# A four-part decoder trunk on one core: 224 bytes in front of the left side of SBUF

## The chip, the core and the metric

The kernel runs on one core of a Trainium2 chip. The metric is the device time of one execution in microseconds (us), the median of several. Engines are named as in the profile: PE (TensorE) does the matmuls, PEld is its weight load, DVE (VectorE) and ACT (ScalarE) work element by element, POOL is GpSimd, and SP issues most DMAs from its queue, in order.

## The reference

One sequence of 1024 tokens, width 1024, float32, goes through two layers. Every layer is a pre-normalised mixer and a pre-normalised SwiGLU FFN (2816 wide), both added to x. The mixer of layer 0 is a forgetting attention of 8 heads beside a causal pooling of 4 channel groups; that of layer 1 is RWKV-7 time mixing: three large projections, three small ones, a recurrence over 16 heads of 64, a norm per head and an output projection.

```python
for layer in range(DEPTH):                       # DEPTH = 2
    h = _rmsnorm(x, mix_norm[layer])
    y = _fox_pool_mixer(h, ...) if layer % 2 == 0 else _rwkv7_time_mix(h, ...)[0]
    x = x + y
    x = x + _swiglu(_rmsnorm(x, ffn_norm[layer]), ffn_w_gate[layer], ffn_w_up[layer], ffn_w_down[layer])
```

## The kernel before, in words

Activations lie transposed, channels on partitions, in tiles of 128 x 512: eight channel blocks for each of two halves of the tokens. A wide product is done in three (`mm3`, L162 to L164): weights and activations are each split into a rounded part and a rest (hi and lo), and hi*hi, hi*lo and lo*hi are added up in PSUM. Each of the three streams a moving tile of 512 columns through a stationary block of 128 x 128 weights. Tiles are named by what they hold: `whi`, `wlo` are weights, `hh` and `hl`, `uh` and `ul`, `h1h` and `h1l`, `mxh` and `mxl`, `gh` and `gl` are the two parts of an activation. `load_part` (L149 to L151) brings weights in: a DMA from the SP queue into `wraw`, a cast on ACT for hi, a subtraction on DVE for lo.

SBUF is used as two stacks that grow towards each other. The left one begins with constants (`setup`: cc, cv, eps, hlast, om, nb, bones) and holds pools opened and closed in order; the right one begins at the far end with `wf`, the pool of weights. Pools of the left side are x0, h (hh, hl of the attention), wl and u (uh, ul: the first FFN and the first dense projection), core and core2 (the recurrence), tail0 and tail1 (hh, hl, gh, gl of the last FFN), and w4, a weight pool for the last stage. Pools of the right side are wf (whi, wlo, wraw for all stages but the last), x1, fox (the attention), t1, m1 (h1h, h1l) and mb (mxh, mxl of the second dense projection). In the listing the side is the second argument of `pool`. A tile's size is rounded up to a multiple of 32 bytes.

The stages in order of time, in the profiled execution: attention and pooling (to about 490 us); the output projection, the first FFN and the first dense projection (490 to 1090); the first recurrence, into whose gaps the rest of the FFN is woven as `fm` from h1 (1090 to 1590); the second dense projection (1590 to 1790); the second recurrence, woven with the last FFN of the first half as `fm` from h and g (1790 to 2290); the last FFN (2290 on). `weave` writes out the order by hand: matmuls of the recurrence stand at fixed places among those of the fill, and PE takes them in that order. A number yielded by `job` says how many matmuls of fill go in between.

`open_core` (L931) sets up a recurrence, twice: it loads the masks (msk), the group constants (gc: 32 columns for sums over a head, 128 for the spread matrix, 1 for a sign), casts the spread matrix to a tile of its own on ACT, and sets the state S. `job` then loads s, k, a, r and v (L958) and uses temporaries of tag t2. Both core pools fill their room to within a few hundred bytes.

Of the kernel before, what the change touches and what calls it, by code (L numbers as in the profile page):

```python
# [9 lines left out]
F32 = mybir.dt.float32  # L10
F32R = mybir.dt.float32r
AF = mybir.ActivationFunctionType
ALU = mybir.AluOpType
# [3 lines left out]
P = 128  # L17
# [38 lines left out]
def make_consts():  # L56
    c = np.zeros((P, NCC), np.float32)
    f = np.zeros((P, NFC), np.float32)
    i = np.arange(P)
    same = (i[:, None] // 64) == (i[None, :] // 64)  # L60
    c[:, CC["ident"]:CC["ident"] + P] = np.eye(P)
    c[:, CC["bones"]:CC["bones"] + P] = same / 64.0
    c[:, CC["ones"]:CC["ones"] + P] = 1.0 / D
    c[:, CC["cent"]:CC["cent"] + P] = np.eye(P) - same / 64.0
    f[:, FC["maskT"]:FC["maskT"] + P] = np.where(i[:, None] > i[None, :], NEG, 0.0)
    f[:, FC["maskQ"]:FC["maskQ"] + P] = np.where(i[None, :] > i[:, None], NEG, 0.0)
    for g, w in enumerate((2, 4, 8, 16)):
        f[:, FC["icnt"] + 16 * g:FC["icnt"] + 16 * g + 16] = 1.0 / np.minimum(np.arange(16) + 1, w)
    return c, f
# [11 lines left out]
def rd(ap):  # L81
    return ap.bitcast(F32)


def setup(ctx, tc, k):
    nc = tc.nc
    k.tc, k.nc = tc, nc
    k.const = ctx.enter_context(tc.tile_pool(name="const", bufs=1))
    k.uid = 0
    k.prio, k.cur = {}, 0  # L90
    k.cc = k.const.tile([P, NCC], F32, tag="cc", name="cc")
    k.cv = k.const.tile([P, NCV], F32, tag="cv", name="cv")
    k.eps = k.const.tile([P, 3], F32, tag="eps", name="eps")
    nc.gpsimd.memset(k.eps[:, 0:1], RMS_EPS)
    nc.gpsimd.memset(k.eps[:, 1:2], GN_EPS)
    nc.gpsimd.memset(k.eps[:, 2:3], 1e-35)
    k.hlast = k.const.tile([P, KT], F32, tag="hlast", name="hlast")
    k.om = k.const.tile([P, 48], F32, tag="om", name="om")
    k.nb = k.const.tile([P, 16], F32, tag="nb", name="nb")
    k.bones = k.const.tile([P, P], F32R, tag="bones", name="bones")  # L100
    k.lag2, k.lag3 = 100000, 100000
# [11 lines left out]
def nm(k, s):  # L113
    k.uid += 1
    return f"{s}_{k.uid}"
# [15 lines left out]
def pst(k, tag, bufs):  # L131
    return k.ps.tile([P, HN], F32, tag=tag, name=nm(k, tag), bufs=bufs)
# [608 lines left out]
class Rwkv:  # L741
# [188 lines left out]
    def open_core(self, cp):  # L930
        k, nc = self.k, self.k.nc  # L931
        self.cp = cp
        self.msk = cp.tile([P, 2, 64], F32, tag="msk", name="msk")
        nc.sync.dma_start(self.msk, self.ins["rconst"])
        self.gc = cp.tile([P, 161], F32, tag="gc", name="gc")
        nc.sync.dma_start(self.gc, self.ins["gconst"])
        self.spread = cp.tile([P, P], F32R, tag="spread", name="spread")
        nc.scalar.copy(self.spread, self.gc[:, 32:160])
        self.rst = cp.tile([P, HN], F32, tag="rst", name="rst")
        nc.gpsimd.memset(self.rst, 1.0)  # L940
        nc.gpsimd.memset(self.rst.rearrange("p (c t) -> p c t", t=64)[:, :, 0:1], 0.0)
        self.S = cp.tile([P, 8, 64], F32, tag="S", name=nm(k, "S"))
        s = self.S.rearrange("p a b -> p (a b)")
        if self.last is None:
            nc.gpsimd.memset(s, 0.0)
        else:
            nc.sync.dma_start(s, self.last)
        self.vc = cp.tile([P, 3, 8], F32, tag="vc", name="vc")
        nc.vector.tensor_scalar(self.vc[:, 0], k.cv[:, CV["k_a"]:CV["k_a"] + 8], -1.0, 1.0, ALU.mult, ALU.add)
        nc.vector.tensor_scalar(self.vc[:, 2], k.cv[:, CV["k_k"]:CV["k_k"] + 8], -1.0, None, ALU.mult)  # L950
        nc.vector.tensor_scalar(self.vc[:, 1], k.cv[:, CV["r_k"]:CV["r_k"] + 8], 64.0, None, ALU.mult)
# [32 lines left out]
    def job(self, grp, half):  # L984
# [4 lines left out]
        k, nc, cp = self.k, self.k.nc, self.cp  # L989
# [210 lines left out]
        rs = self.t2("rs")[:, 0:HN]  # L1200
        nc.scalar.activation(rs, z, AF.Ln, bias=k.eps[:, 1:2])
        nc.scalar.activation(rs, rs, AF.Exp, scale=-0.5)
        hi, both = (self.t2(n, F32R)[:, 0:HN] for n in ("hi", "both"))
        nc.scalar.copy(hi, rs)
        nc.vector.scalar_tensor_tensor(both, rd(hi), self.gc[:, 160:161], rs, ALU.mult, ALU.add)
        yield GY[1]
        for i, p in enumerate(pr):
            q = slice(32 * i, 32 * i + 32)
            rs = pst(k, "o", 2)
# [4 lines left out]
            t = self.t2("gn")[:, 0:HN]  # L1214
# [18 lines left out]
def build(ctx, tc, ins, outs, dbg=None, stop=99):  # L1233
    nc = tc.nc
    k = K()
    setup(ctx, tc, k)
    nc.sync.dma_start(k.cv, ins["cvec"])
    nc.vector.tensor_scalar(k.om, k.cv[:, CV["mu0"]:CV["mu0"] + 48], -1.0, 1.0, ALU.mult, ALU.add)
# [220 lines left out]
def layout(inputs):  # L1459

    f = {n: np.ascontiguousarray(v) for n, v in inputs.items()}
    r = {}

    def wb(w):
        kk, m = w.shape
        return np.ascontiguousarray(w.reshape(kk // P, P, m // P, P).transpose(2, 1, 0, 3).reshape(m // P, P, kk))

    def col(v):
        return v.reshape(-1, P).T

    def wl(w):
        n = w.shape[1]
        return np.ascontiguousarray(w.reshape(KT, P, n).transpose(1, 0, 2).reshape(P, KT * n))

    r["xT"] = np.ascontiguousarray(f["x"][0].T)
    r["consts"], r["fconst"] = make_consts()
    cv = np.zeros((P, NCV), np.float32)

    def put(n, v):
        cv[:v.shape[0], CV[n]:CV[n] + v.shape[1]] = v  # L1480

    for n, v in (("mix0", f["mix_norm"][0]), ("ffn0", f["ffn_norm"][0]), ("mix1", f["mix_norm"][1]), ("ffn1", f["ffn_norm"][1]),
                 ("w0", f["rw_w0"][0]), ("a0", f["rw_a0"][0]), ("k_k", f["rw_k_k"][0]), ("k_a", f["rw_k_a"][0]),
                 ("r_k", f["rw_r_k"][0].reshape(-1)), ("ln_w", f["rw_ln_w"][0]), ("ln_b", f["rw_ln_b"][0]),
                 ("pool_scale", f["hy_pool_scale"][0])):
        put(n, col(v))
    for i in range(6):
        put(f"mu{i}", col(f["rw_mu"][0, i]))
    put("q_gain", np.tile(f["hy_q_gain"][0], 2)[:, None])
    put("k_gain", np.tile(f["hy_k_gain"][0], 2)[:, None])  # L1490
    put("f_bias", f["hy_f_bias"][0][:, None])
    r["cvec"] = cv
    w = f["hy_w_in"][0]
    r["w_in"] = wb(np.concatenate([w[:, 0:2048], w[:, 2056:2568]], axis=1))
    r["wf"] = wl(np.pad(w[:, 2048:2056], ((0, 0), (0, 24))))
    r["pool_w"] = f["hy_pool_w"][0]
    r["w_out"] = wb(f["hy_w_out"][0])
    for n in "rkvo":
        r["w_" + n] = wb(f["rw_w_" + n][0])
    i = np.arange(P) % 64  # L1500
    t = np.arange(64)
    j = np.arange(P) % 32
    gc = np.zeros((P, 161), np.float32)
    gc[:, 0:32] = (np.arange(P)[:, None] // 64 == np.arange(32) % 2) / 64.0
    gc[:, 32:160] = (j[:, None] % 2 == np.arange(P) // 64) & (j[:, None] < 4)
    gc[:, 160] = np.where(j // 2 == 1, -1.0, 0.0)
    r["gconst"] = gc
    r["rconst"] = np.stack([i[:, None] < t, i[:, None] <= t], axis=1).astype(np.float32)

    r["w1"], r["a1"] = wl(f["rw_w1"][0]), wl(f["rw_a1"][0])  # L1510
    r["g1a"], r["g1b"] = wl(f["rw_g1"][0][:, 0:P]), wl(f["rw_g1"][0][:, P:])
    r["w2"], r["a2"] = np.tile(f["rw_w2"][0], (2, 1)), np.tile(f["rw_a2"][0], (2, 1))
    r["g2a"], r["g2b"] = np.ascontiguousarray(f["rw_g2"][0][0:P]), np.tile(f["rw_g2"][0][P:], (3, 1))
    for l in range(2):
        r[f"wg{l}"] = wb(f["ffn_w_gate"][l])
        r[f"wu{l}"] = wb(f["ffn_w_up"][l])
        r[f"wd{l}"] = np.ascontiguousarray(f["ffn_w_down"][l].reshape(NFB, P, 8, P).transpose(2, 1, 0, 3))
    return r
# [29 lines left out]
```

## Time and profile before

| | us |
|---|---|
| median of 3 runs (lowest, highest) | 2719.55 (2719.53, 2722.38) |
| profiled execution, its own time | 2725.7 |
| its span | 2723.9 |

Over the span PE is busy 98%, PEld 76%, DVE 63%, ACT 48%, POOL 2%. In the profile a busy PE counts each matmul from its start to its modelled end; neighbours overlap, so the distance from start to start says how fast they follow each other, not the duration. Idle time in a row is the engine's idle time just before the instructions of that row, and behind the arrow stands what ended it.

### The profile page before, as it was taken

The numbers are of one execution on the slowest core, as the hardware profiler recorded it, in microseconds if no ns is written. First come the engines' busy times: TensorE is split into PE (matmuls) and PEld (weight loads), VectorE is DVE, ScalarE is ACT, GpSimd is POOL, SyncE is SP. The second block draws the span as 40 slices with busy tenths as digits, with TensorE's granted clock in tenths as the row PEclk, the third lists the DMA queues.
The fourth block names the chain that finished last, engine by engine and source line by source line (L and its number), as shares of the span: only waits on it lengthen the run. The fifth ranks groups of instructions, "written<-read, shape, count | busy, mean of one in ns | idle before, by whom it ended". The sixth has DMA issues, their size and how long they took to land.

```text
span 2723.9 us, 40262 instructions
## 1 busy us (share of the span) xinstructions
PE 2665.5 (98%) x15368; PEld 2080.5 (76%) x15368; DVE 1725.1 (63%) x2940; ACT 1297.9 (48%) x2297; POOL 50.0 (2%) x139
## 2 busy tenths in 40 slices
PE   9999999999999999999999999999999999999999
PEld 6777778778888777777777677777777777788887
DVE  7777684653336655975995676569769856544443
ACT  7555564442224766534644467655445344333232
POOL 1000000000001000000000000000000000000000
PEclk9999999999999999999999999999999999999999
DMA  4111131233333445423533534454344236333332
GB/s 134 57 51 57 41 96 51 82 93 94 94 96 112 159 164 179 132 88 95 175 93 98 185 105 154 163 184 128 90 136 136 86 98 201 104 97 97 97 97 93
DMA packets 170241, 306.11 MB, mean 112 GB/s; under 512 B 18608, under 2 KB 25904, under 8 KB 170048
## 3 DMA queue, kind: packets, MB, share of 16 engines
q1 hardware_dynamic: 156224, 278.38, 32.8%
q10 hardware_dynamic: 13824, 25.17, 2.5%
q8 instruction: 120, 1.97, 0.3%
q14 instruction: 73, 0.60, 0.1%
HBM read 257.04 MB, written 46.43 MB: 111 GB/s over the span
## 4 chain that ended last, share of the span: by engine, by line
PE 82%; DVE 11%; ACT 3%; DMA 2%; issue 2%; SPq 0%; ACTq 0%; DVEq 0%
PE mm L162 17%; PE mm L163 16%; PE mm L164 16%; PE fm L162 7%; PE fm L164 6%; PE fm L163 6%; DVE wlo L151 2%; PE mm L174 1%; DVE nu L1109 1%; DVE pd L1107 1%; PE s L1057 1%; PE o L1174 1%; PE s L1162 1%; PE s L1168 1%; PE o L1187 1%
## 5 line engine op out<-in xcount | busy, mean ns | idle before, releaser
L150 ACT CAST whi<-wraw 128x512 fp32r<-128x512 f32 x738 | 453.1, 616 | 891.6 <-PE mm L163 493.0
L151 DVE TENSOR_TENSOR wlo<-wraw,whi 128x512 fp32r<-128x512 f32 x738 | 500.9, 683 | 455.9 <-ACT whi L150 445.5
L162 PE MATMUL mm<-hh,whi 128*128 128x512 f32 x864 | 345.1, 401 | 5.8 <-ACT hh L354 5.7
L164 PE MATMUL mm<-hh,wlo 128*128 128x512 f32 x864 | 340.4, 394 | 0.0
L163 PE MATMUL mm<-hl,whi 128*128 128x512 f32 x864 | 339.5, 394 | 0.0
L164 PE MATMUL mm<-uh,wlo 128*128 128x512 f32 x728 | 287.3, 395 | 1.4 <-DVE wlo L151 1.4
L162 PE MATMUL mm<-uh,whi 128*128 128x512 f32 x728 | 287.7, 397 | 0.9 <-DVE x L1315 0.9
L163 PE MATMUL mm<-ul,whi 128*128 128x512 f32 x728 | 287.5, 396 | 0.0
L162 PE MATMUL fm<-h1h,whi 128*128 128x512 f32 x528 | 220.7, 418 | 14.0 <-DVE sg L725 9.9
L163 PE MATMUL fm<-h1l,whi 128*128 128x512 f32 x528 | 210.1, 398 | 0.1
L164 PE MATMUL fm<-h1h,wlo 128*128 128x512 f32 x528 | 209.7, 397 | 0.5 <-DVE wlo L151 0.5
L162 PEld LDWEIGHTS mm<-hh,whi 128*128 128x128 f32 x864 | 162.8, 189 | 42.6 <-ACT hh L354 6.5
L164 PEld LDWEIGHTS mm<-hh,wlo 128*128 128x128 f32 x864 | 162.8, 188 | 35.9 <-DVE wlo L151 0.6
L163 PEld LDWEIGHTS mm<-hl,whi 128*128 128x128 f32 x864 | 163.2, 189 | 33.6 <-DVE hl L259 1.5
L162 PE MATMUL fm<-hh,whi 128*128 128x512 f32 x416 | 174.5, 420 | 3.2 <-ACT hh L258 2.7
L164 PE MATMUL fm<-hh,wlo 128*128 128x512 f32 x416 | 167.9, 404 | 0.0
L163 PE MATMUL fm<-hl,whi 128*128 128x512 f32 x416 | 167.7, 403 | 0.2 <-DVE hl L259 0.2
L162 PEld LDWEIGHTS mm<-uh,whi 128*128 128x128 f32 x728 | 136.4, 188 | 38.7 <-issue 3.5
L163 PEld LDWEIGHTS mm<-ul,whi 128*128 128x128 f32 x728 | 136.6, 188 | 35.8 <-issue 1.1
L164 PEld LDWEIGHTS mm<-uh,wlo 128*128 128x128 f32 x728 | 136.5, 188 | 35.0 <-DVE wlo L151 2.2
L704 DVE TENSOR_TENSOR x<-mm,x 128x512 f32<-128x512 f32 x96 | 66.2, 692 | 122.8 <-PE mm L164 122.5
L162 PEld LDWEIGHTS fm<-h1h,whi 128*128 128x128 f32 x528 | 100.4, 190 | 48.1 <-DVE sg L725 12.3
(338 smaller groups left out, 4642.5 us busy)
## 6 DMA issues: line engine op xcount, KB each, us to landing
wraw<-in_wg_dram SPq DMA_DIRECT2D x176, 256.0 KB, 2.8
wraw<-in_wu_dram SPq DMA_DIRECT2D x176, 256.0 KB, 2.7
wraw<-in_wd_dram SPq DMA_DIRECT2D x176, 256.0 KB, 2.7
wraw<-in_w_in_dram SPq DMA_DIRECT2D x52, 256.0 KB, 2.9
x<-in_xT_dram SPq DMA_DIRECT2D x32, 256.0 KB, 4.6
x<-x SPq DMA_DIRECT2D x32, 256.0 KB, 3.6
wraw<-in_w_k_dram SPq DMA_DIRECT2D x32, 256.0 KB, 2.8
wraw<-in_w_v_dram SPq DMA_DIRECT2D x32, 256.0 KB, 3.0
```

Source lines behind the costliest of these rows:

```text
L150: k.nc.scalar.copy(hi[0:p, 0:n], raw[0:p, 0:n])
L151: k.nc.vector.tensor_tensor(lo[0:p, 0:n], raw[0:p, 0:n], rd(hi[0:p, 0:n]), ALU.subtract)
L162: nc.tensor.matmul(out, wh, xh, start=(first and i == 0), stop=False)
L163: nc.tensor.matmul(out, wh, xl, start=False, stop=False)
L164: nc.tensor.matmul(out, wl, xh, start=False, stop=(last and i == n - 1))
L174: k.nc.tensor.matmul(out[n * q:n * q + n], w[:, n * j:n * j + n], xs[j], start=c == 0, stop=c + g == len(xs), tile_position=(0, n * q))
L704: nc.vector.tensor_tensor(X[half][m], o, X[half][m], ALU.add)
L1057: nc.tensor.matmul(scs[h][:, 128 * c:128 * c + 128], bk[HS[h], 4 * b + c], ZL[h][HS[h], i, 4 * b + c], start=True, stop=True)
L1107: nc.vector.tensor_tensor(pv, nu[:, j + 1:32, j:j + 1].broadcast_to([P, n, j]), nu[:, j:j + 1, 0:j].broadcast_to([P, n, j]), ALU.mult)
L1109: nc.vector.tensor_tensor(nu[:, j + 1:32, 0:j], nu[:, j + 1:32, 0:j], pv, ALU.add)
L1162: nc.tensor.matmul(z[HS[h], i], ZL[h][:, i, c, 0:64], SV[h][:, i, c], start=True, stop=True)
L1168: nc.tensor.matmul(u[HS[h], i], XR[HS[h], i, c, 0:64], zs[HS[h], i], start=True, stop=True)
```

## The change

The eps tile, of which three columns are used, grows from 3 to 64 columns: from 12 bytes, rounded up to 32, to 256. All tiles of the left side behind it (hlast, om, nb, bones and all left pools) move up by 224 bytes; cc, cv and the right side stay. To make room in the core pools, gc keeps 33 columns of its 161 (from 672 bytes after rounding to 160), and the 128 columns of the spread matrix come by a DMA of their own into a temporary of tag t2, from which ACT casts them. The sign column moves from 160 to 32, in the constants and where it is read.

```diff
-    k.eps = k.const.tile([P, 3], F32, tag="eps", name="eps")
+    k.eps = k.const.tile([P, 64], F32, tag="eps", name="eps")
...
-        self.gc = cp.tile([P, 161], F32, tag="gc", name="gc")
-        nc.sync.dma_start(self.gc, self.ins["gconst"])
+        self.gc = cp.tile([P, 33], F32, tag="gc", name="gc")
+        nc.sync.dma_start(self.gc, self.ins["gconst"][:, 0:33])
         self.spread = cp.tile([P, P], F32R, tag="spread", name="spread")
-        nc.scalar.copy(self.spread, self.gc[:, 32:160])
+        t = self.t2("spread")[:, 0:P]
+        nc.sync.dma_start(t, self.ins["gconst"][:, 33:161])
+        nc.scalar.copy(self.spread, t)
...
-        nc.vector.scalar_tensor_tensor(both, rd(hi), self.gc[:, 160:161], rs, ALU.mult, ALU.add)
+        nc.vector.scalar_tensor_tensor(both, rd(hi), self.gc[:, 32:33], rs, ALU.mult, ALU.add)
...
-    gc[:, 32:160] = (j[:, None] % 2 == np.arange(P) // 64) & (j[:, None] < 4)
-    gc[:, 160] = np.where(j // 2 == 1, -1.0, 0.0)
+    gc[:, 33:161] = (j[:, None] % 2 == np.arange(P) // 64) & (j[:, None] < 4)
+    gc[:, 32] = np.where(j // 2 == 1, -1.0, 0.0)
```

## Rows read from the trace of the kernel before

**Rows 1.** The page: busy time of each engine, and the chain that ended last
```profile
PE 2665.5 (98%) x15368; PEld 2080.5 (76%) x15368; DVE 1725.1 (63%) x2940; ACT 1297.9 (48%) x2297; POOL 50.0 (2%) x139
...
PE 82%; DVE 11%; ACT 3%; DMA 2%; issue 2%; SPq 0%; ACTq 0%; DVEq 0%
```
**Rows 2.** Windows by stage: length, busy us (instructions) PE PEld DVE ACT POOL, clock, DMA share, GB/s
```profile
0.00:490.00 490.00, 477.11 (x2217) 376.17 (x2218) 347.85 (x696) 280.86 (x510) 16.64 (x46) 1.00 0.22 68
490.00:1090.00 600.00, 595.76 (x2584) 468.37 (x2583) 311.04 (x479) 277.31 (x467) 13.67 (x26) 1.00 0.38 122
1090.00:1590.00 500.00, 479.33 (x3886) 364.90 (x3885) 381.36 (x654) 235.96 (x438) 8.99 (x30) 0.98 0.39 123
1590.00:1790.00 200.00, 197.02 (x835) 149.77 (x834) 114.93 (x175) 128.64 (x214) 0.15 (x2) 0.99 0.46 149
1790.00:2290.00 500.00, 486.26 (x3969) 368.34 (x3968) 378.28 (x649) 244.13 (x456) 10.59 (x35) 0.99 0.42 130
2290.00:2724.00 434.00, 430.04 (x1886) 352.99 (x1884) 191.64 (x290) 131.04 (x215) 0.00 (x0) 1.00 0.32 100
```
**Rows 3.** Timeline, PE, first FFN: start us, us, instruction; first and last of 19
```profile
699.74 0.40 PE L163 MATMUL mm<-ul,whi 128*128 128x512 f32 x1
...
703.94 0.40 PE L163 MATMUL mm<-ul,whi 128*128 128x512 f32 x1
```
**Rows 4.** Timeline, PE, second dense projection: first and last of 13
```profile
1739.64 0.39 PE L162 MATMUL mm<-mxh,whi 128*128 128x512 f32 x1
...
1742.36 0.39 PE L162 MATMUL mm<-mxh,whi 128*128 128x512 f32 x1
```
**Rows 5.** Timeline, PE, last FFN: first and last of 13
```profile
2449.67 0.39 PE L162 MATMUL mm<-hh,whi 128*128 128x512 f32 x1
...
2452.39 0.39 PE L162 MATMUL mm<-hh,whi 128*128 128x512 f32 x1
```
**Rows 6.** The page's groups: count | busy us, mean ns | idle before, releaser
```profile
L162 PE MATMUL fm<-h1h,whi 128*128 128x512 f32 x528 | 220.7, 418 | 14.0 <-DVE sg L725 9.9
L163 PE MATMUL fm<-h1l,whi 128*128 128x512 f32 x528 | 210.1, 398 | 0.1
L164 PE MATMUL fm<-h1h,wlo 128*128 128x512 f32 x528 | 209.7, 397 | 0.5 <-DVE wlo L151 0.5
...
L162 PE MATMUL fm<-hh,whi 128*128 128x512 f32 x416 | 174.5, 420 | 3.2 <-ACT hh L258 2.7
L164 PE MATMUL fm<-hh,wlo 128*128 128x512 f32 x416 | 167.9, 404 | 0.0
L163 PE MATMUL fm<-hl,whi 128*128 128x512 f32 x416 | 167.7, 403 | 0.2 <-DVE hl L259 0.2
```
**Rows 7.** Groups of 0:490, 490:1090, 1790:2290 (two), 2290:2724 (two): the middle product
```profile
L163 PE MATMUL mm<-hl,whi 128*128 128x512 f32 x441 | 175.0, 398 | 0.0
...
L163 PE MATMUL mm<-ul,whi 128*128 128x512 f32 x728 | 287.5, 396 | 0.0
...
L163 PE MATMUL fm<-hl,whi 128*128 128x512 f32 x324 | 130.6, 403 | 0.0
...
L163 PE MATMUL fm<-gl,whi 128*128 128x512 f32 x132 | 52.5, 398 | 0.0
...
L163 PE MATMUL fm<-gl,whi 128*128 128x512 f32 x44 | 17.3, 397 | 0.0
...
L163 PE MATMUL fm<-hl,whi 128*128 128x512 f32 x24 | 9.5, 395 | 0.0
```
**Rows 8.** Timeline of SP's queue at the first opening and the second
```profile
1063.54 0.42 SPq L936 DMA_DIRECT2D gc<-in_gconst_dram  x1
1064.05 0.38 SPq L958 DMA_DIRECT2D ld<-s  x1
...
1793.72 0.45 SPq L947 DMA_DIRECT2D S<-S  x1
1795.97 0.33 SPq L958 DMA_DIRECT2D ld<-s  x1
```

## The prediction

> **What bounds the kernel now.** I read the busy line and the chain of the page first [rows 1]: TensorE is busy 98% of the span and holds 82% of the chain that ended last, VectorE 11%. So the spacing of its matmuls is the time, unless a stage says otherwise. The table by stage comes next [rows 2]; the reader is to see that TensorE is busy 477 to 480 of 490 to 500 us even in the stages in which the other engines do most (attention, 0:490; the two recurrences, 1090:1590 and 1790:2290), and 596 of 600 and 430 of 434 in the dense stages.
>
> "Busy" is not "at its best" here, and the third view, the timeline, shows it. In the first FFN the wide matmul (128x512) starts every 233.3 ns: 18 steps in 703.94 - 699.74 = 4.20 us [rows 3]. In the second dense projection it starts every 226.7 ns: 12 steps in 2.72 us [rows 4], and in the last FFN again every 226.7 ns [rows 5]. The instruction is the same each time, from the same line, at the same granted clock (1.00 in 490:1090 and 2290:2724 [rows 2]), with no idle time in front of it. What differs is where the two operands lie. In rows 3 the moving tile uh comes from a pool of the left side and the weights whi and wlo from a pool of the right. In rows 4 both come from the right, in rows 5 both from the left (the last stage has weight pool w4, on the left). By the sizes in the code all tiles of one side that hold a wide operand (2048 bytes each; the eight x tiles of a pool, 2080 bytes each, add up to a multiple of 256) stand at one place modulo 256, and the two sides 32 bytes apart: the pad is 256 - 32. So operands at equal places step at 226.7 ns and operands 32 bytes apart at 233.3: 6.6 ns, 2.8%.
>
> The same pair is to be seen where matmuls fill the gaps of a recurrence. There I go by durations, as the starts are mixed with short matmuls: fm from h1 (right side, right weights) takes 418, 398 and 397 ns for its three products, fm from h (left side, right weights) 420, 403 and 404 [rows 6]. That is 2, 5 and 7 ns, on average 4.7 ns. (In the dense stages the duration falls with the spacing, 396 [rows 7] against 389 [rows 4, 5].)
>
> **The change part by part.** The pad moves every left tile after it by 224 bytes. Left moving tiles then stand at the weights' place modulo 256; left weights under left tiles and right under right keep their relation, as both or none move. gc shrinks by 512 bytes, a multiple of 256, so core tiles behind it end at the same new place as the rest. Which matmuls change class, by the rows that count the middle one of three products [rows 7], each times 3:
> - first FFN and first dense projection, 728 x 3 = 2184, at 6.6 ns: 14.4 us. TensorE is continuous there [rows 2], so all of it arrives.
> - end of the FFN, 2290 on, (24 + 44) x 3 = 204, at 6.6 ns: 1.3 us, all of it.
> - attention, 441 x 3 = 1323. No row shows such a matmul at equal places there; the bounds are 0 and 6.6 ns. I take the 4.7 of rows 6, the nearest row in which matmuls are mixed with other work: 6.2 us.
> - second recurrence, (324 + 132) x 3 = 1368, at 4.7 ns: 6.4 us.
> - the rest of fm from h, 416 - 324 - 24 = 68, x 3 = 204, at 4.7 ns: 1.0 us.
>
> Of the last three not all arrives. In the second recurrence VectorE is busy 378 of 500 us [rows 2], and fm from h waits little now (3.2 us over the whole span, 2.7 of them for the split of hh [rows 6]); but the first recurrence, whose fill has the quick placing already, waited 14.0 us on its L162 [rows 6], 9.9 of them for the SwiGLU product of VectorE at L725. I read that as what is late next once the fill is quicker, and let half of the 6.4 arrive: 3.2 us. In attention and the rest I let seven eighths arrive, 6.3 of 7.2, as TensorE idles 13 of 490 us there [rows 2].
>
> Of what matmuls without a wide left operand do, little is known: products with a constant tile ahead of the pad (cc stays where it is) change their distance. By the code there are 4 jobs x 4 head pairs x 16 = 256 short products with cent and as many transposes with ident. They could gain or lose; by 6.6 ns on each this is 3.4 us either way, and as they read an eighth of the columns I take 0.
>
> The other edit costs something. Each open of a core puts one more transfer into SP's queue, between gc and the loads of the recurrence. In the first opening SP issues gc at 1063.54 and ld<-s at 1064.05 [rows 8]: one more issue is about 0.5 us by which ld<-s and all behind it in the queue come later. The target is a t2 tile, which must be free: at the second opening the nearest row of such a wait is ld<-s, 2.3 us behind S<-S with an issue of 0.45 us, thus some 1.8 us of waiting. So 0.5 to 2.3 us each, 0 if the fill (f1's matmuls) covers it. I take 0.5 twice, 1.0 us. ScalarE's copy into spread waits for the new transfer in place of gc's and has the scan's results queued behind it; the scan waits for ld<-s, which is issued later, so the copy holds nothing up.
>
> Sum: 14.4 + 1.3 + 3.2 + 6.3 - 1.0 = 24.2 us off. The profiled execution took 2725.7 us (span 2723.9 and 1.8 around it), so 2701.5, a factor of 0.9911. The runs have their median at 2719.55, 0.2% below that execution; by the same factor they come to 2695.4. I say 2695.
>
> [...]
>
> **The rivals.**
> - Only the continuous stages gain. The mixed stages are bound by the chain of VectorE and ScalarE, and quicker fill is waited away. For it: the 14.0 us of the first recurrence. Against: 82% of the chain is TensorE. 14.4 + 1.3 = 15.7, less 1.0 to 4.6 for the openings, 11 to 15 us off: 2705 to 2708.5.
> - All arrives, at the full 6.6 ns: 2184 + 204 + 1323 + 1368 + 204 = 5283 x 6.6 = 34.9 us off, 2685.
> - The places modulo 256 have nothing to do with it; the two speeds go with the stage or the pool. For it: each class is seen in stages of its own. Against: rows 4 and 5 agree to the tenth of a ns with operands on opposite sides of the memory, other tiles and other DMA shares (0.46 and 0.32 [rows 2]). Then 0 to +5 us: 2720 to 2724.
> [...]
>
> **How the numbers follow.** The forecast 0.61 (2690 to 2701); only the continuous stages 0.20; all at the full rate 0.10; no effect of the place 0.05; the clock 0.04. The range reaches from 2687 (most of the full gain) to 2708 (nearly all of the second case): 0.61 of the first, some 0.17 of the second and some 0.04 of the third, about 0.8. What a measurement of this kernel can tell from no change is 0.2%, 5.4 us. Faster by more: 0.61 + 0.20 + 0.10 = 0.91; within: 0.05; slower: 0.04.
>
> **What would show it.** Right: in the first FFN the starts of L162 to L164 step by 226.7 ns and uh, ul come to 389 to 390 ns; fm from h takes what fm from h1 does; the stage that ended at 1090 ends some 20 us earlier, the last one changes by 1 to 2 us. The first recurrence is as long as before. If uh still steps at 233 ns the main step is wrong; if it steps at 227 and the span does not follow, the handing on is. If ld<-s comes more than 2 us behind gc, the price of the transfer is. [...]

## The result, and the profile after

| | us |
|---|---|
| before, on the same chip: median of 4 runs (the three of before and one more) | 2720.97 |
| after: median of 4 runs (lowest, highest) | 2701.28 (2699.79, 2703.13) |
| ratio, 95% interval | 0.9923 [0.9904, 0.9942] |
| profiled execution of after, its own time | 2699.79 |

The change made the kernel faster by 0.8%, 19.7 us by the medians. The profiled execution went from 2725.7 to 2699.79 us, 25.9 less.

The page of after, its busy line and the chain that ended last, beside [rows 1]:

```profile
PE 2632.5 (98%) x15368; PEld 2072.6 (77%) x15368; DVE 1725.1 (64%) x2940; ACT 1298.7 (48%) x2297; POOL 49.4 (2%) x139
...
PE 77%; DVE 14%; ACT 3%; DMA 3%; issue 3%; SPq 0%; DVEq 0%; ACTq 0%
```

TensorE runs the same 15368 matmuls and is busy 33.0 us less, its weight loads 7.9 less, and the other engines are within 1 us of before. Its share of the chain fell from 82 to 77%, VectorE's rose from 11 to 14%: the kernel is still bound by TensorE, a little less so.

The windows by stage of after (columns as in [rows 2]):

```profile
0.00:490.00 490.00, 476.30 (x2232) 377.91 (x2233) 350.81 (x701) 281.57 (x511) 16.64 (x46) 1.00 0.21 69
490.00:1090.00 600.00, 595.72 (x2705) 478.78 (x2704) 325.76 (x502) 287.63 (x484) 13.33 (x28) 1.00 0.40 125
1090.00:1590.00 500.00, 478.00 (x3844) 365.00 (x3844) 379.81 (x651) 237.94 (x439) 8.04 (x27) 0.99 0.39 123
1590.00:1790.00 200.00, 194.76 (x820) 146.45 (x818) 111.07 (x170) 130.16 (x218) 2.28 (x8) 0.99 0.50 162
1790.00:2290.00 500.00, 483.41 (x3995) 371.69 (x3996) 381.51 (x654) 240.49 (x448) 9.08 (x30) 0.99 0.41 127
2290.00:2698.00 408.00, 404.27 (x1779) 332.78 (x1777) 176.19 (x266) 120.90 (x198) 0.00 (x0) 1.00 0.33 98
```

TensorE is about as full as before in every stage (0.8 to 2.9 us less in those with other work), and in 490:1090 it gets 2705 matmuls done where it did 2584 [rows 2]. The timeline of the first FFN shows why; first and last of 19 wide matmuls, beside [rows 3]:

```profile
700.05 0.39 PE L163 MATMUL mm<-uh,whi 128*128 128x512 f32 x1
...
704.13 0.39 PE L163 MATMUL mm<-uh,whi 128*128 128x512 f32 x1
```

That is 18 steps in 4.08 us: 226.7 ns each, where it was 233.3. The page's groups that answer to [rows 6 and 7]:

```profile
L163 PE MATMUL mm<-uh,whi 128*128 128x512 f32 x728 | 283.5, 391 | 0.9 <-DVE x L1318 0.9
L165 PE MATMUL mm<-uh,wlo 128*128 128x512 f32 x728 | 283.1, 389 | 1.2 <-DVE wlo L152 1.2
...
L163 PE MATMUL fm<-h1h,whi 128*128 128x512 f32 x528 | 218.7, 415 | 14.8 <-DVE sg L726 10.6
L165 PE MATMUL fm<-h1h,wlo 128*128 128x512 f32 x528 | 208.7, 396 | 0.5 <-DVE wlo L152 0.5
L164 PE MATMUL fm<-h1l,whi 128*128 128x512 f32 x528 | 208.5, 395 | 0.1
...
L163 PE MATMUL fm<-hh,whi 128*128 128x512 f32 x416 | 172.4, 414 | 3.5 <-ACT hh L259 2.8
L164 PE MATMUL fm<-hl,whi 128*128 128x512 f32 x416 | 164.5, 396 | 0.2 <-DVE hl L260 0.2
L165 PE MATMUL fm<-hh,wlo 128*128 128x512 f32 x416 | 164.6, 396 | 0.0
```

The fill from h now takes what the fill from h1 takes: 414, 396, 396 ns against 415, 395, 396. Its waits stayed (3.5 us, 3.2 before).

To see where the 26 us went I compared the start of each matmul with that of the same matmul, by its place in PE's order, in the trace of before. The length of a stage is then the distance between the same two matmuls in every kernel. The kernels of the experiments give more values for each stage. "Apart" are those whose left side stands 32 or 128 to 224 bytes off the right one (before, p0, p192, d128_160, d192_16); "equal" are four that keep the pad of 224 bytes (after, t32, lo32, after2). In the first recurrence, the second dense projection and the last FFN most operands are at equal places in both; what changes there is 28, 175 and 52 products of fill from h and g. Kernels that change the last FFN itself are left out of its two rows.

| stage, us | before | after | mean of the kernels apart | mean of those equal | difference |
|---|---|---|---|---|---|
| attention | 483.9 | 480.4 | 484.1 (5) | 480.9 (4) | -3.2 |
| output projection, first FFN, first dense projection | 571.7 | 557.4 | 571.1 (5) | 557.5 (4) | -13.6 |
| first recurrence | 518.7 | 515.1 | 516.5 (5) | 516.2 (4) | -0.3 |
| second dense projection | 211.0 | 210.3 | 211.2 (5) | 210.5 (4) | -0.7 |
| second recurrence | 476.9 | 473.9 | 476.9 (5) | 474.2 (4) | -2.7 |
| start of the last FFN | 79.1 | 78.6 | 79.5 (3) | 78.6 (2) | -0.9 |
| last FFN | 372.5 | 372.3 | 372.5 (3) | 372.3 (2) | -0.2 |

The differences add up to 21.6 us. The profiled pair differs by 4 us more, most of it in the first recurrence (3.6 in place of 0.3), and that goes with the granted clock: TensorE ran part of the stage at 0.50, as the windows 1085:1090 and 1190:1195 of before show. There six steps of the fill from h1, from 1193.30 to 1195.86, take 427 ns each; the median step of that fill at 1.00 is 227. Two longer windows of before (columns as in [rows 2]):

```profile
1060.00:1110.00 50.00, 47.94 (x301) 37.34 (x300) 40.00 (x65) 31.42 (x57) 1.89 (x6) 0.93 0.55 171
...
1160.00:1210.00 50.00, 45.46 (x414) 36.07 (x413) 39.39 (x69) 19.27 (x34) 0.00 (x0) 0.90 0.26 77
```

The same windows of after:

```profile
1060.00:1110.00 50.00, 45.63 (x363) 34.66 (x364) 48.67 (x79) 29.94 (x56) 1.05 (x4) 1.00 0.46 148
...
1160.00:1210.00 50.00, 45.94 (x570) 35.66 (x569) 33.81 (x48) 19.29 (x36) 0.00 (x0) 0.97 0.27 80
```

With 0.50 as the lower level, a mean clock of 0.93 over 50 us is 7 us at it, 0.90 is 10. By the comparison matmul by matmul after gains 1.9 us around the first of these stretches and 2.6 around the second, and loses 0.9 in the rest of the stage. Over the span the time at 0.50 adds up to 44 us in the profile of before and 23 in that of after, and it goes from 21 to 39 us among the kernels below, so single executions scatter widely. But scatter is not all of it: the mean granted clock is 0.9938 over the 29 runs of before beside the experiments and 0.9942 over the 10 of p0, against 0.9952 over the 17 of after, after2, fox and fox2. By twice the missing share of the span that is 32 to 34 us at the lower level against 26. By 427 against 227 ns TensorE loses a little under half of such a time, so, as an estimate, up to 3 or 4 of the 20 us or so gained can have come with the clock; why kernels with the pad were granted more, no run shows. No profile shows the lower level between 14 and 1084 us (before and after have 1.00 in 14:500 and 500:1060, and before then 0.52 in 1084:1091), so the 16.8 us of the first two stages are free of it.

### The profile page after: what moved, and what is told of

It reads as the page before. It is cut to its first block, busy times and chain, and to the rows that moved or that the text cites. A ratio compares the mean times of both kernels' runs of the same rounds, so it can differ in the third digit from the quotient of the medians.

```text
span 2698.0 us, 40269 instructions
## 1 busy us (share of the span) xinstructions
PE 2632.5 (98%) x15368; PEld 2072.6 (77%) x15368; DVE 1725.1 (64%) x2940; ACT 1298.7 (48%) x2297; POOL 49.4 (2%) x139
## 4 chain that ended last, share of the span: by engine, by line
PE 77%; DVE 14%; ACT 3%; DMA 3%; issue 3%; SPq 0%; DVEq 0%; ACTq 0%
PE mm L163 16%; PE mm L164 16%; PE mm L165 16%; PE fm L163 6%; PE fm L164 5%; PE fm L165 5%; DVE wlo L152 2%; PE mm L175 1%; DVE nu L1112 1%; DVE pd L1110 1%; DVE ZL L1068 1%; DMA wraw<-in_wd_dram 1%; DMA wraw<-in_wu_dram 1%; ACT whi L151 1%; PE o L1177 1%
## 5 line engine op out<-in xcount | busy, mean ns | idle before, releaser
L163 PE MATMUL mm<-hh,whi 128*128 128x512 f32 x864 | 343.7, 400 | 6.7 <-ACT hh L355 6.2
L163 PE MATMUL mm<-uh,whi 128*128 128x512 f32 x728 | 283.5, 391 | 0.9 <-DVE x L1318 0.9
L163 PE MATMUL fm<-h1h,whi 128*128 128x512 f32 x528 | 218.7, 415 | 14.8 <-DVE sg L726 10.6
L163 PEld LDWEIGHTS mm<-hh,whi 128*128 128x128 f32 x864 | 162.5, 188 | 43.1 <-ACT hh L355 6.9
L163 PE MATMUL fm<-hh,whi 128*128 128x512 f32 x416 | 172.4, 414 | 3.5 <-ACT hh L259 2.8
L163 PEld LDWEIGHTS mm<-uh,whi 128*128 128x128 f32 x728 | 136.5, 188 | 34.6 <-issue 2.7
L163 PEld LDWEIGHTS fm<-h1h,whi 128*128 128x128 f32 x528 | 99.5, 189 | 48.7 <-DVE sg L726 13.3
```

The lines of the kernel that those rows point to most:

```text
L163: nc.tensor.matmul(out, wh, xh, start=(first and i == 0), stop=False)
```

## The experiments

All but the last two groups ask what makes the step short. Each kernel is the changed one with the edit shown; times of the kernel before are from the same chip.

**Is it the pad, or the other edit?** p0 takes the pad away and keeps the spread transfer and the smaller gc.

```diff
-    k.eps = k.const.tile([P, 64], F32, tag="eps", name="eps")
+    k.eps = k.const.tile([P, 3], F32, tag="eps", name="eps")
```

> The changed kernel with the pad taken out again (eps 3 columns wide) and the other edit left in: gc narrow, the spread matrix by a transfer of its own. Left tiles stand 32 bytes off the weights, as before. If the place is what counts: uh in the first FFN steps at 233.3 ns, the time is that of the kernel before plus 0 to 1 us for the added transfers, ratio 1.000. If the gain came with the other edit (less room taken by gc, another order in SP's queue, fewer stretches at half clock): the time is that of the changed kernel, ratio 0.992, although uh steps at 233.3.

2724.14 us (10 runs) against 2724.44 before, ratio 0.9997 [0.9987, 1.0006]. The timeline of its first FFN, 18 steps in 4.20 us, 233.3 ns again:

```profile
699.27 0.39 PE L163 MATMUL mm<-uh,whi 128*128 128x512 f32 x1
...
703.47 0.39 PE L163 MATMUL mm<-uh,whi 128*128 128x512 f32 x1
```

The whole gain is the pad's, and the other edit costs nothing that can be measured.

**Is it the side, or the place?** t32 leaves the pad and puts 32 bytes in front of the tiles of the last stage, whose moving tiles and weights are both on the left. They are then 32 bytes apart on one side.

```diff
     c_l, lp = pool("tail1")
+    lp.tile([P, 8], F32, tag="pad", name="pad")
```

> The changed kernel, with a tile of 32 bytes in front of pool tail1 (hh, hl, gh, gl of the last FFN), so that in the last stage alone the moving tiles stand 32 bytes off the weights of pool w4, both on the left. If the distance counts: mm from hh and gh steps at 233.3 ns in place of 226.7; (384 + 176) x 3 = 1680 steps x 6.6 ns = 11.1 us more than the changed kernel, all in the last 420 us, ratio to the kernel before 0.9964. If what counts is that operands lie on different sides: no change in the last stage, 226.7 ns, ratio 0.992.

2712.66 us (4 runs), ratio to before 0.9959 [0.9944, 0.9974]; the last FFN took 382.6 in place of 372.3 us. Its timeline, 18 steps in 4.20 us:

```profile
2449.29 0.39 PE L163 MATMUL mm<-hh,whi 128*128 128x512 f32 x1
...
2453.49 0.39 PE L163 MATMUL mm<-hh,whi 128*128 128x512 f32 x1
```

So 32 bytes bring the 233.3 ns to operands of one side, other things equal, and the stage loses 10.3 us. Side and stage fall as explanations.

**Which weights count?** lo32 does the same for the lo weights alone: whi at the moving tiles' place, wlo 32 bytes from it.

```diff
-    hi, lo = ((pool or k.wp).tile([P, w], F32R, tag=tag + i, name=nm(k, tag + i), bufs=bufs or k.wbufs) for i in ("hi", "lo"))
+    wp = pool or k.wp
+    hi = wp.tile([P, w], F32R, tag=tag + "hi", name=nm(k, tag + "hi"), bufs=bufs or k.wbufs)
+    if wp is getattr(k, "padlo", None):
+        wp.tile([P, 56], F32, tag="pad", name="pad")
+        k.padlo = None
+    lo = wp.tile([P, w], F32R, tag=tag + "lo", name=nm(k, tag + "lo"), bufs=bufs or k.wbufs)
...
     c_w, wp4 = pool("w4")
+    k.padlo = wp4
     c_l, lp = pool("tail1")
+    lp.tile([P, 8], F32, tag="pad2", name="pad2")
```

> The changed kernel, with wlo of pool w4 moved down against everything else in the last stage, so that the moving tile stands 32 bytes above wlo (the slow distance) and level with whi. If the moving stream is slowed by the load of the next weights: of three steps only the one from L164 to L165 is 233 ns long (hl streams while wlo is loaded), the others 226.7; 560 steps x 6.6 = 3.7 us over the changed kernel. If it is slowed by the weights that it runs through itself: only the step that starts at L165 is long. If any place off the common one slows all: all three at 233, 11 us.

One run, 2709.22 us; last FFN 379.1 us, 6.8 more than in after. Timeline, 18 steps in 4.16 us, 231.1 ns:

```profile
2448.88 0.39 PE L168 MATMUL mm<-hh,whi 128*128 128x512 f32 x1
...
2453.04 0.39 PE L168 MATMUL mm<-hh,whi 128*128 128x512 f32 x1
```

Over the stage the three steps differ: from hh,whi to hl,whi 226.7 ns, from hl,whi to hh,wlo 235.0, from hh,wlo to the next hh,whi 231.7. The step that is longest is that of hl, which runs through weights at its own place while the 32 bytes distant wlo is being loaded (in the trace of after a load of wlo and the product from gl beside it both start at 2449.28 us, and take 0.19 and 0.39). So the load of the next weights beside the running stream matters. Whether the 231.7 comes from the running stream's own weights or is carried over from the step before isn't told apart; neither figure that I had expected for the stage came out.

**Which distances are quick?** p192 pads 192 bytes (distance 32 the other way). The three others have two distances each: one in the first FFN by the size of eps, one in the last by a pad in tail1 as in t32 (96 and 160 bytes) or, in d192_16, by gh and gl starting 16 bytes into larger tiles.

```diff
# p192, d64_96, d128_160, d192_16: distances 224 (-32), 64, 128, 192 in the first FFN
-    k.eps = k.const.tile([P, 64], F32, tag="eps", name="eps")
+    k.eps = k.const.tile([P, 56], F32, tag="eps", name="eps")    # 16, 32, 48
# d64_96, d128_160: 96, 160 in the last FFN
+    lp.tile([P, 24], F32, tag="pad", name="pad")                 # 40
# d192_16: 16 for gh and gl of the last FFN
...
+        hi, lo = (pool.tile([P, n + 64], F32R, tag=tag, name=nm(k, tag + i), bufs=bufs)[:, 4:4 + n] for i in "hl")
```

> The changed kernel with a pad of 192 bytes: left tiles stand 32 bytes below the weights' place modulo 256 (before: 32 above). If only the distance counts, whatever its sign: uh steps at 233.3 ns and the time is that of the kernel before, 2720. If the sign counts, the step is another one, between 216 and 240 ns; at 226.7 ns the time would be 2701.

> Two distances in one kernel: a pad of 32 bytes on the left (left tiles 64 bytes above the right weights modulo 256: first FFN) and 96 bytes in front of tail1 (moving tiles 96 above the weights: last FFN). If only equal places modulo 256 are quick: uh steps at 233.3 ns and hh of the last FFN at 233.3; 2720 + 11 = 2731. If the rule is modulo 64: uh at 226.7 and hh of the last FFN (96 = 32 modulo 64) at 233.3; 2701 + 11 = 2712. If the step grows with the distance: uh over 234, hh of the last FFN higher still.

> As the one before, with distances of 128 bytes (first FFN) and 160 (last FFN). Equal places modulo 256 alone quick: 233.3 and 233.3 ns, 2731. Modulo 64 or 128: uh at 226.7, last FFN (160 = 32) at 233.3, 2712. Modulo 256 with a step that grows with the distance: the highest here.

> A distance of 192 bytes in the first FFN, and in the last FFN gh and gl alone (the down projection) 16 bytes above the weights, hh and hl level with them. Equal places modulo 256 alone quick: uh at 233.3 ns; gh at 226.7 if 16 bytes lie within one place, else at 233.3 or between; hh at 226.7 as in the changed kernel. Modulo 64: uh at 226.7, gh off.

One run each: 2722.87, 2721.58, 2734.7 and 2725.01 us (before 2724.44 for the first, 2722.46 for the others). The mean step at each distance, over its stage, steps of 250 ns and more left out as waits:

| bytes apart | 0 | 16 | 32 | 64 | 96 | 128 | 160 | 192 | 224 |
|---|---|---|---|---|---|---|---|---|---|
| ns | 226.7 | 231.6 | 233.3 | 229.7 | 233.4 | 233.2 | 234.3 | 233.3 | 233.3 |

Of each kernel one timeline of 18 steps, which can lie up to 1 ns off the mean. p192, first FFN, 4.20 us:

```profile
700.70 0.40 PE L163 MATMUL mm<-uh,whi 128*128 128x512 f32 x1
...
704.90 0.40 PE L163 MATMUL mm<-uh,whi 128*128 128x512 f32 x1
```

d64_96, first FFN, 64 bytes, 4.12 us:

```profile
700.87 0.39 PE L163 MATMUL mm<-uh,whi 128*128 128x512 f32 x1
...
704.99 0.39 PE L163 MATMUL mm<-uh,whi 128*128 128x512 f32 x1
```

d128_160, last FFN, 160 bytes, 4.22 us:

```profile
2449.15 0.39 PE L163 MATMUL mm<-hh,whi 128*128 128x512 f32 x1
...
2453.37 0.39 PE L163 MATMUL mm<-hh,whi 128*128 128x512 f32 x1
```

d192_16, last FFN, 16 bytes, 4.17 us:

```profile
2606.41 0.40 PE L163 MATMUL mm<-gh,whi 128*128 128x512 f32 x1
...
2610.58 0.39 PE L163 MATMUL mm<-gh,whi 128*128 128x512 f32 x1
```

Only equal places give the whole gain. 16 bytes already cost 4.9 of the 6.5 to 7.6 ns, 64 bytes cost 3.0, and the loss doesn't grow with the distance: that the step repeats every 64 bytes falls, and so does a cost that rises with distance. The place by itself doesn't count either: in before, d192_16, p192 and after, hh of the last FFN and its weights stand together 0, 160, 192 and 224 bytes further, and the step is 226.7 to 226.9 ns in all four.

**Why did attention gain only 3.2 us, where 5.4 were forecast?** One theory: the attention's own products, whose tiles aren't at equal places, disturb those beside them. fox aligns the tiles that come behind ncumT and fc (ph, pl and others).

```diff
-        ncumT = ap_.tile([P, 8, 8], F32, tag="ncumT", name="ncumT")
+        ncumT = ap_.tile([P, 10, 8], F32, tag="ncumT", name="ncumT")[:, 0:8]
...
-    fc = ap_.tile([P, 320], F32, tag="fc", name="fc")
+    fc = ap_.tile([P, 368], F32, tag="fc", name="fc")
...
-    nc.sync.dma_start(fc, ins["fconst"][:, 0:320])
+    nc.sync.dma_start(fc[:, 0:320], ins["fconst"][:, 0:320])
```

> The changed kernel with the attention's own tiles moved: fc 192 bytes longer and ncumT 64, so that ph, pl, ak, aq and av of the right side stand at the weights' place too (before and in the changed kernel 64 bytes off). The attention gained 3.3 us by the change where 5.4 were forecast. If what holds it back is that its own products of ph and pl still stand off and disturb the steps of hh between them: the step of hh from L163 and L165 falls from 230 to 232 ns to 227 to 228 and the first 465 us get 1.5 to 2.5 us shorter, 2699. If it is the change of streams itself (short products, waits for VectorE): no change there, 2701.

2697.49 us (4 runs), ratio to before 0.9906 [0.9889, 0.9923]; attention 479.9 us against 480.4, and the mean steps of hh and hl there fall by some 0.5 ns, to 229 to 230. That is less than the theory asks for: it falls.

The other theory: a run of wide products needs some steps after a product of another shape until it steps quickly. The trace of after shows it in attention; first, second, sixth and last of a run of nine, and the product that follows it:

```profile
257.83 0.45 PE L163 MATMUL mm<-hh,whi 128*128 128x512 f32 x1
258.12 0.39 PE L164 MATMUL mm<-hl,whi 128*128 128x512 f32 x1
...
259.05 0.39 PE L165 MATMUL mm<-hh,wlo 128*128 128x512 f32 x1
...
259.73 0.39 PE L165 MATMUL mm<-hh,wlo 128*128 128x512 f32 x1
259.96 0.40 PE L556 MATMUL o<-ph,VH 128*128 128x512 f32 x1
```

From the second to the sixth start four steps take 0.93 us, 232.5 ns each; from there four take 0.91, 227.5. Two kernels put such a product where none was: in the last FFN of the changed kernel, after every 6 (cut6) or 24 (cut24) wide products, one of 128 columns whose result nothing reads.

```diff
+        if k.wp is getattr(k, "cut", None):
+            k.ncut += 1
+            if k.ncut % 2 == 0:                  # cut24: % 8
+                nc.tensor.matmul(k.scr[:, 0:128], wl, xh[:, 0:128], start=True, stop=True)
         yield 3
...
+    k.cut, k.ncut, k.scr = wp4, 0, pst(k, "scr", 1)
```

> The changed kernel; in the last FFN's stage (pool w4) one more short product (128 columns, same weights and moving tile, into a PSUM bank that nobody reads) behind every 6 wide ones. All operands stand at equal places and no other engine is waited for. If a run of wide products reaches its quick step only after some steps, and a product of another kind sets it back: the steps in each group of six fall from 231 to 233 ns behind the short one towards 227 to 228, mean 229 to 230. If the slow first steps in attention and recurrence come from the other engines' work there: all wide steps but the one beside the short product stay at 226.7.

> As the one before with a short product behind every 24 wide ones. If the quick step has to be reached again: steps of 231 to 233 ns behind the short product, 226.7 from about the eighth on, mean of the wide steps 227.5 to 228. If not: 226.7 throughout but for the step beside the short product.

One run each: 2742.72 and 2712.88 us, against 2703.39 for the changed kernel on that chip. The timeline of cut24 around two of its short products:

```profile
2500.39 0.22 PE L169 MATMUL scr<-hh,wlo 128*128 128x128 f32 x1
2500.45 0.45 PE L163 MATMUL mm<-hh,whi 128*128 128x512 f32 x1
2500.73 0.39 PE L164 MATMUL mm<-hl,whi 128*128 128x512 f32 x1
...
2502.34 0.39 PE L165 MATMUL mm<-hh,wlo 128*128 128x512 f32 x1
...
2505.97 0.22 PE L169 MATMUL scr<-hh,wlo 128*128 128x128 f32 x1
```

After the short one and the longer step behind it (0.28 us), seven steps take 1.61 us, 230 ns each, and the 16 after those 3.63, 226.9. Over the stage, with the few steps over 300 ns left out, the steps behind a short product have means of 284, 231, 236, 228, 233, 231 and 226.5 ns, and 226.5 to 227.0 from there; in cut6 284, 231, 236, 229, 232, 231, and the next short one comes. A cut so costs 57 ns for the short product itself, 57 in the step behind it and 25 in the five after that, in both kernels: 74 cuts at 139 ns are 10.3 us (measured 9.5), 296 are 41.1 (39.3). The theory stands: places being equal, a short run does not get the short step. The way there was not the expected one: the steps don't fall evenly, and the five in cut6 have a mean of 231.7 ns, where 229 to 230 was expected.

**Is there a better kernel, and does the result repeat?** after2 is the changed kernel again and fox2 is fox again, both on one chip.

> The changed kernel once more, for its ratio beside the next one on the same chip: 0.990 to 0.994 of the kernel before.

> The changed kernel with ph, pl, ak, aq and av of the attention at the weights' place too, once more. In the look before it took 0.5 us less in the attention (480.4 to 479.9 us). If that is all: 0 to 1 us under the run of the changed kernel beside it, not to be told apart; if the 4 us between the medians of the two (2701.3 and 2697.5, of different runs) are real: ratio 0.9985 between them.

after2 2703.39 us (5 runs), ratio to before 0.9925 [0.9911, 0.9938]; fox2 2701.0 (4 runs), 0.9917 [0.9904, 0.9931]. The result repeats. The two intervals overlap, so aligning the attention's tiles too isn't told apart from the changed kernel, and no version here clearly beats it.

## Why the prediction was right

I said 2695 us, between 2687 and 2708, for a median of 2719.55; the measured median is 2701.28. For the profiled execution the sum said 2701.5, and it took 2699.79, with some 3 us from the clock in its favour; that this figure was met so closely is in part luck. By steps:

- **The step of 6.6 ns.** Right. uh and ul step at 226.7 ns, and the stage lost 13.6 us (14.3 in the profiled pair) of the 14.4 forecast. p0, t32 and the table of distances show the cause: the place modulo 256, not the side, the pool or the stage. lo32 puts nothing but the lo weights off the common place, and the step of the product beside which they are loaded grows from 226.7 to 235.0 ns. What in the memory makes the place count, no run shows. Two readings were looser than the prediction told them: rows 3 are of L163 and rows 4 and 5 of L162, not of one line, and times given to 0.01 us fix a step over 12 or 18 of them only to 0.8 and 0.6 ns. The means over the stages of before bear them out, 233.3 ns in the first FFN and 226.7 in the last.
- **End of the FFN, 1.3.** Right in size: the start of the last FFN lost 0.9 and its long part 0.2.
- **Second recurrence, 3.2.** Measured 2.7. Its two factors were both off and made up for each other in part. By the starts in the two traces, the steps of fill inside this stage shrank by 4.7 us together and not 6.4 (that its many short runs are the reason is read from their lengths and not tried); somewhat more than half of that arrived. The clock is at work in this stage too (0.99 over it in before and after, with 0.50 in 1797:1799 of after) and kernels of one kind lie up to 3 us apart in it, so the 2.7 is known to a microsecond or so.
- **Attention and the rest, 6.3.** This is the term that was mis-sized. Attention was to bring 7/8 of 6.2, that is 5.4, and brought 3.2. The step that failed is "I take the 4.7 of rows 6, the nearest row in which matmuls are mixed with other work": those rows are means over the recurrences, where runs are longer. Counted in the trace of after over the stages of the table, 662 of 1403 steps of fill in the first recurrence come behind at least 12 wide products in a row, but only 180 of 1109 steps in attention. There the mean step is 231 to 233 ns up to the fourth product of a run, 227 to 230 from the fifth to the eighth and 227 from the thirteenth; in before it is 231 to 234.5 throughout. The 1070 steps of attention that hold no wait shrank by 3.2 us together, 3.0 ns each, where the prediction took 4.7 for all 1323 products. That is what was gained: the size of the step and the number that have it were off, and not the share that arrives. The rest, 0.9, came about as forecast: its 203 products step at 227.7 ns in place of 232.7.
- **The second transfer, -1.0.** Too dear: p0, which has it and not the pad, is within 0.03% of before. SP's queue at the two openings of after, beside [rows 8]:

```profile
1045.86 0.48 SPq L937 DMA_DIRECT2D gc<-in_gconst_dram  x1
1046.44 0.98 SPq L940 DMA_DIRECT2D spread<-in_gconst_dram  x1
1047.47 0.42 SPq L961 DMA_DIRECT2D ld<-s  x1
...
1772.00 0.43 SPq L940 DMA_DIRECT2D spread<-in_gconst_dram  x1
1774.00 0.33 SPq L950 DMA_DIRECT2D S<-S  x1
1774.43 0.39 SPq L961 DMA_DIRECT2D ld<-s  x1
```

At the first, ld<-s comes 1.61 us behind gc, 1.1 later than in [rows 8]; the fill covers it. At the second the wait that stood in front of ld<-s [rows 8] now stands in front of S<-S: from the start of the transfer before it to ld<-s it is 2.43 us, where it was 2.25 from S<-S. The new transfer took the place of a part of an old wait.
- **The first recurrence as long as before.** Right by the kernels' means (0.3 us); the 3.6 of the profiled pair go with the clock (0.98 in 1090:1590 of before, 0.99 of after). The short products against constants, put at nothing, can't be made out: half of them are in this stage.
- **The rivals.** "Only the continuous stages" (11 to 15 us off) is out, though not by far: attention and second recurrence gave 5.9 us between them. "All at the full rate" (34.9) is out. "The place has no effect" is out by p0 and t32. The 0.04 for the clock came to nothing: no run shows a quicker fill bringing a lower granted clock. The recurrences' mean clock is 0.99 and 0.99, where it was 0.98 and 0.99 [rows 2], and over all runs it was higher with the pad, 0.9952 against 0.9938.

The forecast of the median, 24.2 us off, is 4 to 5 more than measured: 2.2 from attention, the rest from terms of under 1 us and from scatter of the same size.

## What to carry to other kernels

Where TensorE is the bound and "busy" is near 100%, read the distance from start to start of equal matmuls stage by stage: two values for one instruction (here 233.3 and 226.7 ns) show that something other than the program's order sets them, and here a pad of 224 bytes was worth 0.8%. A gain per step that is read from long runs, or from a mean over long and short ones, should be weighed by the length of the runs in the stage it is applied to (cut6: 231.7 ns on the mean of five steps behind the first, where long runs have 226.7). An edit made only to find room for another is best tried by itself, as p0 does, before a price is put on it.

## What the runs showed of the hardware that was not expected

- Equal places modulo 256 are the only quick ones tried. 16 bytes apart make it 231.6 ns, 64 bytes 229.7, and 32, 96, 128, 160, 192 and 224 bytes 233.2 to 234.3, against 226.7. These are means: at 96 bytes the steps from hh,whi, hl,whi and hh,wlo are 232.1, 237.2 and 230.8 ns, though all three are the same distance apart.
- The quick step has a run-up. After one product of 128 columns it is reached at the seventh step (cut24), and a kernel that cuts after every six products never reaches it (231.7 ns on the mean of the five steps behind the first).
- With only the lo weights displaced (lo32) the step of the stream beside whose run they are loaded is the longest, 235.0 ns, while the step between the two products that share whi stays at 226.7.
- Open: whether anything brings the step below 226.7 ns, as no distance tried does; and whether longer runs of fill in attention would bring the 2 us that are missing there, which wasn't tried; and why the clock was granted a little more with the pad (0.9952 against 0.9938).
